# Gates and up projection of an encoder layer as seven products of halves

## The chip, the cores and the metric

One Trainium2 chip, one core of it. The time is the device time of one execution of the whole program in microseconds (us). TensorE (PE) does the matrix products, VectorE (DVE) and ScalarE (ACT) the arithmetic around them, GpSimd (POOL) some of it and the software DMA queue, SyncE (SP) issues most of the loads.

## The reference

Two groups of 256 tokens (512 in all, model width 1024) go through one encoder layer. Cut to what matters here:

```python
proj = rms_norm(x, norm1_g) @ w_in          # q, k, v of three branches, and three gates
qa, ka, va, qb, kb, vb, qm, ga, gb, gm = split(proj)
...                                         # attention branches oa, ob, om
merged = (sigmoid(ga) * (oa @ w_branch_a)
          + sigmoid(gb) * (ob @ w_branch_b)
          + sigmoid(gm) * (om @ w_branch_m))
x = x + merged @ w_out
h2 = rms_norm(x, norm2_g)
x = x + square(relu(h2 @ w_up)) @ w_down    # w_up 1024 x 4096, w_down 4096 x 1024
y = rms_norm(x, final_norm_g)
```

Each gate is a product 512 x 1024 by 1024 x 1024, the up projection one by 1024 x 4096. All of it is float32.

## The kernel before

**Precision by halves.** A float32 operand is split into a rounded part hi (ACT copies it into the type float32r) and a rest lo (DVE subtracts hi). `mm3` adds three products into one PSUM bank: hi by hi, hi by lo, lo by hi. Every weight tile `raw` or `blk` (128 x 1024 floats, 512 KB) so costs one ACT copy and one DVE subtraction before PE can use it.

**Units.** The program is a list of units that `run` emits in order; each has a function and the weights that it needs. Weights are fetched `ahead` weight tiles before their use (3 in the stages that matter here). The `lo` subtractions of a fetched tile are put into a list `lows`, which is emitted at the start of the next unit; what reads a product out of PSUM waits in a list `later`, which `flush` emits after the next product's matmuls. PE, ACT, DVE keep the order in which they were emitted; the order of DMAs on the SP and POOL queues is set by the scheduler.

**Gate stage.** Attention ends, then for each of eight blocks of 128 output features (`ff`): gate A and gate B, each `fm` with 8 contraction blocks of 128, 24 matmuls 128 x 512 (tokens are the 512 columns); then `branches`, the three branch products against OA, OB and OM (12, 6 and 12 matmuls), each multiplied by its gate on DVE and summed on POOL. The memory gate GM was computed earlier. `merge` splits the sums (tiles `mg`) for the output projection `out_proj`, which adds the residual and makes H, the normalised input of the MLP (up to the factor 1/rms, which comes in at the end).

**MLP.** The hidden width 4096 is walked in 8 columns `c` of 512. `up` makes a column of hidden features in 4 products of 24 matmuls 128 x 512, cut into 8 half units; in turns with them stand the seven products (P1, P2, Q5, Q6, P7, Q3, Q4) of the down projection of the column before, which is already written as seven products of halves instead of eight (12 matmuls 128 x 512 each). Its operands are sums of quarters of the weight: a tile T is changed in place by three accumulating DMAs on the POOL queue (`accum_op=add`), a tile C by one. Operands of tokens are made by `form` (DVE differences, ACT hi, DVE lo). Results go into accumulators by DVE (`acc`). Two products of a pair (P1 and P2, Q5 and Q3, P7 and Q4) share PSUM banks: the second adds to what the first left, after the first has been read.

In the profile almost every instruction of PE, ACT and DVE has line 72 (a helper); tiles tell them apart: `x` the normalised tokens, `g`, `q` gates, `w` weight halves, `h` H, `f` forms, `u` hidden features.

Of the kernel before, what the change touches and what calls it, by code (L numbers as in the profile page):

```python
# [16 lines left out]
P = 128  # L17
# [60 lines left out]
def encoder_kernel(ctx: ExitStack, tc: tile.TileContext, a: dict, out: bass.AP):  # L78
# [20 lines left out]
    def h2(s="h", dt=F32):  # L99
        return sb.tile([P, T], dt, tag="h2", name=nm(s), bufs=20)  # L100
# [10 lines left out]
    def f(x):  # L111
        return x.bitcast(F32)
# [86 lines left out]
    def fm(w, X, o):  # L199

        n = len(X)
        for k in range(n):
            c = slice(k * P, (k + 1) * P)
            mm3(o, w[0][:, c], w[1][:, c], X[k][:, 0], X[k][:, 1], k == 0, k == n - 1)
# [554 lines left out]
        unit(flush)  # L759


    MG, wb, sg = [], [], {}

    def gate(w, ff, br):
        p = bank()
        fm(w, X, p)
        g = h2("g")
        A.activation(g, p, AF.Sigmoid)
        sg[ff, br] = g

    def branches(w, *more):
        ff = len(MG)
        if more:
            wb[:] = more
        A.activation(GM[ff], GM[ff], AF.Sigmoid)
        sg[ff, 2] = GM[ff]
        c0 = (ff % 4) * 256
        parts = ((w[0][:, :512], w[1][:, :512], OA), (wb[0][0][:, c0:c0 + 256], wb[0][1][:, c0:c0 + 256], OB),
                 (w[0][:, 512:], w[1][:, 512:], OM))
        for br, (wh, wl, O) in enumerate(parts):  # L780
            p = bank()
            fm((wh, wl), O, p)
            V.tensor_tensor(sg[ff, br], p, sg[ff, br], op=ALU.mult)
        eng = V if ff == KD - 1 else G
        eng.tensor_tensor(sg[ff, 0], sg[ff, 0], sg[ff, 1], op=ALU.add)
        eng.tensor_tensor(sg[ff, 0], sg[ff, 0], sg[ff, 2], op=ALU.add)
        MG.append(sg[ff, 0])

    M = []

    def merge(*ks):
        for k in ks:
            x = s4("mg")
            A.activation(x[:, 0], MG[k], AF.Copy)
            (V, G)[k % 2 if k < KD - 1 else 0].tensor_tensor(x[:, 1], MG[k], f(x[:, 0]), op=ALU.subtract)
            M.append(x)

    for ff in range(KD):
        for br in range(2):
            unit(lambda w, ff=ff, br=br: gate(w, ff, br), (a["w_g"][ff, br],))  # L800
        if ff == KD - 1:
            unit(lambda: merge(*range(KD - 1)))
        unit(branches, (a["w_bam"][ff],), *([(a["w_bb"][ff // 4],)] if ff % 4 == 0 else []))


    unit(lambda: merge(KD - 1))


    X1, H = [], []

    def out_proj(w):
        ff = len(H)
        r = h2("xr")
        A.dma_start(r, a["xT"][:, ff])
        p = bank()
        fm(w, M, p)
        V.tensor_tensor(r, p, r, op=ALU.add)
        X1.append(r)
        x = s4("h")
        A.activation(x[:, 0], r, AF.Copy, scale=gains[:, 2, ff:ff + 1])  # L820
        V.scalar_tensor_tensor(x[:, 1], r, gains[:, 2, ff:ff + 1], f(x[:, 0]), op0=ALU.mult,
                               op1=ALU.subtract)
        H.append(x)

    for ff in range(KD):
        unit(out_proj, (a["w_o"][ff],))

# [74 lines left out]
    def load_blocks(c):  # L902

        if c in blocks:
            return
        t = {n: block_tile() for n in "T2BC"}
        for n, b in (("T", "11"), ("2", "21"), ("C", "12"), ("B", "22")):
            SP.dma_start(t[n], block(c, b))
        G.dma_start(t["C"], block(c, "22"), accum_op=ALU.add)
        blocks[c] = t  # L910

    def parts(c, n):

# [17 lines left out]
    def form(c, name):  # L931
# [9 lines left out]
        if name in ("P1", "P2", "Q4"):  # L941
            src = {"P1": A11, "P2": A12, "Q4": A22}[name]
        elif name == "Q5":
            src = forms[c, "S1"] = less(A21, A22)
        elif name == "Q6":
            src = forms[c, "S2"] = less(A11, forms.pop((c, "S1")))
        elif name == "P7":
            src = less(A11, A21)
        else:
            src = less(A12, forms.pop((c, "S2")))  # L950
# [8 lines left out]
    def add_to(k, i, p, op=ALU.add):  # L959
        if (k, i) in acc:  # L960
            V.tensor_tensor(acc[k, i], acc[k, i], p, op=op)
        else:
# [1 line left out]
            A.activation(acc[k, i], p, AF.Copy, scale=1.0 if op == ALU.add else -1.0)  # L964


    PRODUCTS = dict(P1=("T12", "a", "V", -1), P2=("2", "a", "11", 1), Q5=("T22", "d", "G", 1),
                    Q6=("T21", "c", "V", 1), P7=("C", "e", "G", -1), Q3=("B", "d", "12", 1), Q4=("T", "e", "21", 1))

    def product(w, c, name):  # L970
        _, bk, to, sign = PRODUCTS[name]
# [86 lines left out]
    unit(mlp_pool)  # L1058
    ORDER = ("P1", "P2", "Q5", "Q6", "P7", "Q3", "Q4")


    SUMMED = {1: ("12", "12"), 2: ("11", "11"), 3: ("21", "21"), 4: ("12", "V"), 5: ("21", "V", 1), 6: ("22", "G")}

    def make(c, n):
        unit(lambda: form(c, ORDER[n]))

    for c in range(NC):
        for h in range(8):
            ff, half = 4 * c + h // 2, h % 2
            unit(lambda *w, ff=ff, half=half: up(w[0] if w else None, ff, half), *([(a["w_up"][ff],)] if half == 0 else []))  # L1070
            if c == 0:
                unit(lambda h=h: turn_x1(h % 4, h // 4))
            if h == 1 and c < NC - 1:
                unit(lambda c=c: load_blocks(c))
            if h == 7 and c == NC - 2:
                unit(fetch_x1)
            if c == NC - 1 and h == 6:
                unit(lambda: ahead.__setitem__(0, 2))
            if c == NC - 1 and h in SUMMED:
                unit(lambda n=SUMMED[h]: later.append(lambda: combine(*n)))  # L1080
            if c and h < 7:
                for n in ((1, 2) if h == 0 else (h + 2,)):
                    if n < 7:
                        make(c - 1, n)
                unit(lambda w, c=c - 1, n=ORDER[h]: product(w, c, n), (parts(c - 1, PRODUCTS[ORDER[h]][0]),))
        if c == 0:
            unit(inv_ms)
            unit(lambda: ahead.__setitem__(0, 3))
        if c < NC - 1:
            make(c, 0)  # L1090
    unit(lambda *w: (kept.update({(0, 0): w[0], (1, 0): w[1]}), last_down(0, (0, 1))),
         *[(block(NC - 1, n),) for n in ("11", "21")])
    unit(lambda: later.append(lambda: combine("22", "V")))
# [84 lines left out]
```

## Time and profile before

| | us |
|---|---|
| median of 3 runs | 858.68 (857.31 to 859.06) |
| profiled execution | 859.08 |
| its span (first to last instruction) | 857.3 |
| PE busy in the span | 844.4 |
| DVE busy | 462.8 |
| ACT busy | 397.1 |
| POOL busy | 216.0 |

An instruction's duration includes the time until its last result is written, and the next one of the same engine begins before that; what one more instruction costs in a row is the distance between starts. The granted TensorE clock is 1.0 of full speed from 60 us on.

### The profile page before, as it was taken

How to read it: one execution, taken by the hardware profiler on the slowest of the kernel's cores; microseconds unless marked ns; L12 is line 12 of the kernel's file. 1: busy time of each engine (PE TensorE's matmuls, PEld its weight loads, DVE VectorE, ACT ScalarE, POOL GpSimd, SP SyncE). 2: the span in 40 equal slices, each digit the busy share in tenths (PEclk: the TensorE clock that was granted, in tenths of full speed). 3: DMA queues.
4: the chain of work that ended last, by engine and by line, in shares of the span. 5: the costliest groups of instructions: out<-in, count | busy, mean ns of one | idle time of the engine just before them, and what ended most of it. 6: DMA issues, size and time to landing. Idle time of an engine off the chain costs nothing.

```text
span 857.3 us, 10785 instructions
## 1 busy us (share of the span) xinstructions
PE 844.4 (99%) x4080; PEld 703.8 (82%) x4080; DVE 462.8 (54%) x737; ACT 397.1 (46%) x690; POOL 216.0 (25%) x161
## 2 busy tenths in 40 slices
PE   9999999999999999999999999999999999999996
PEld 7788998888888888888888788888888888888885
DVE  6575535465452311423435542465767666767895
ACT  6455545565554333222323227564445353545453
POOL 2314554656556543211123000000000000000001
PEclk9999999999999999999999999999999999999998
DMA  8343122324241228432322445374747465645322
GB/s 284 115 119 109 62 99 86 98 63 115 85 119 64 75 74 286 132 99 86 110 99 74 147 147 161 110 204 107 205 109 208 111 185 121 178 120 172 75 75 98
DMA packets 47468, 106.87 MB, mean 125 GB/s; under 512 B 19358, under 2 KB 19604, under 8 KB 47416
## 3 DMA queue, kind: packets, MB, share of 16 engines
q1 hardware_dynamic: 39992, 85.69, 30.2%
q0 software_dynamic: 4256, 14.73, 9.7%
q10 hardware_dynamic: 3168, 5.77, 2.0%
q8 instruction: 32, 0.52, 0.3%
q14 instruction: 20, 0.16, 0.1%
HBM read 101.93 MB, written 4.24 MB: 124 GB/s over the span
## 4 chain that ended last, share of the span: by engine, by line
PE 84%; DVE 8%; ACT 5%; issue 2%; DMA 1%; POOL 0%; POOLq 0%; SPq 0%; DVEq 0%; ACTq 0%
PE ps L72 77%; PE sc L72 3%; PE o L72 2%; DVE w L72 2%; PE tp L72 2%; ACT w L72 2%; DVE f L72 1%; ACT sp L72 1%; DVE sp L72 1%; DMA mr<-in_memT 1%; ACT f L72 1%; DVE sq L72 0%; ACT r L72 0%; DVE mg L72 0%; DVE acc L72 0%
## 5 line engine op out<-in xcount | busy, mean ns | idle before, releaser
L72 PE MATMUL ps<-x,w 128*128 128x512 f32 x1080 | 252.5, 391 | 0.0
L72 PEld LDWEIGHTS ps<-x,w 128*128 128x128 f32 x1080 | 201.0, 188 | 41.3
L72 PE MATMUL ps<-h,w 128*128 128x512 f32 x768 | 184.5, 391 | 0.0
L72 PEld LDWEIGHTS ps<-h,w 128*128 128x128 f32 x768 | 143.7, 188 | 29.5
L72 PE MATMUL ps<-w,f 128*128 128x512 f32 (+1 forms) x696 | 164.1, 387 | 1.3 <-DVE acc L72 1.0
L72 DVE TENSOR_TENSOR w<-raw,w 128x1024 fp32r<-128x1024 f32 (+1 forms) x79 | 96.4, 1223 | 115.3 <-ACT w L72 115.2
L72 PEld LDWEIGHTS ps<-w,f 128*128 128x128 f32 x696 | 128.7, 188 | 29.9 <-issue 3.4
L72 ACT ACTIVATE w<-raw 128x1024 fp32r<-128x1024 f32 (+2 forms) x116 | 119.7, 1036 | 21.9 <-DMA raw<-in_w_mem 7.5
L161 POOL TENSOR_TENSOR w<-raw,w 128x1024 fp32r<-128x1024 f32 (+1 forms) x37 | 87.3, 2361 | 120.1 <-ACT w L72 94.9
L72 DVE TENSOR_TENSOR w<-blk,w 128x1024 fp32r<-128x1024 f32 x49 | 59.5, 1224 | 47.7 <-ACT w L72 47.6
L923 POOL DMA_DIRECT2D blk<-in_w_dn x21 | 18.1, 864 | 240.2 <-DVE w L72 240.2
L72 ACT ACTIVATE w<-blk 128x1024 fp32r<-128x1024 f32 x49 | 50.7, 1047 | 15.4 <-DMA blk<-in_w_dn 15.4
L72 DVE TENSOR_TENSOR acc<-acc,ps 128x512 f32<-128x512 f32 x82 | 52.9, 682 | 2.9 <-PE ps L72 2.9
L72 ACT ACTIVATE f<-f 128x512 fp32r<-128x512 f32 x28 | 17.7, 633 | 75.4 <-DVE f L72 75.4
L72 ACT ACTIVATE sp<-sp,st 128x256 f32<-128x256 f32 (+1 forms) x48 | 25.8, 538 | 57.7 <-DVE st L72 57.7
L72 ACT ACTIVATE g<-ps 128x512 f32<-128x512 f32 x16 | 9.6, 598 | 88.4 <-PE ps L72 88.4
L72 DVE TENSOR_TENSOR sum<-o,lo 64x256 f32<-64x256 f32 x24 | 10.0, 417 | 66.5 <-ACT lo L72 66.3
L72 PE MATMUL ps<-mg,w 128*128 128x512 f32 x192 | 44.2, 391 | 1.5 <-ACT mg L72 0.9
L72 PEld LDWEIGHTS ps<-mg,w 128*128 128x128 f32 x192 | 36.0, 188 | 9.6 <-ACT mg L72 1.3
L72 ACT ACTIVATE r<-ps 128x512 f32<-128x512 f32 x32 | 18.9, 591 | 50.7 <-PE ps L72 50.7
L72 PE MATMUL ps<-w,x 128*128 128x384 f32 (+1 forms) x192 | 39.9, 363 | 0.0
L469 POOL TENSOR_TENSOR sp<-sp,st 128x512 f32<-128x512 f32 (+1 forms) x32 | 36.7, 1147 | 6.5 <-DVE st L72 3.6
(146 smaller groups left out, 959.2 us busy)
## 6 DMA issues: line engine op xcount, KB each, us to landing
raw<-in_w_up SPq DMA_DIRECT2D x32, 512.0 KB, 4.7
blk<-in_w_dn SPq DMA_DIRECT2D x28, 512.0 KB, 6.7
blk<-in_w_dn POOLq DMA_DIRECT2D x28, 512.0 KB, 5.7
raw<-in_w_g SPq DMA_DIRECT2D x24, 512.0 KB, 3.3
raw<-in_w_b SPq DMA_DIRECT2D x12, 512.0 KB, 3.3
raw<-in_w_bam SPq DMA_DIRECT2D x8, 512.0 KB, 3.3
raw<-in_w_o SPq DMA_DIRECT2D x8, 512.0 KB, 3.2
raw<-in_w_mem SPq DMA_DIRECT2D x7, 512.0 KB, 3.3
```

The costliest lines, as they stand in the source:

```text
L72: return self.tc.keep_in_program_order(method(*args, **kw))
L161: sub[0].tensor_tensor(lo[:, c], raw[:, c], f(hi[:, c]), op=ALU.subtract)
L469: G.tensor_tensor(s[:, :, :w], s[:, :, :w], st[:, 6:8].unsqueeze(2).to_broadcast([P, 2, w]), op=ALU.mult)
L923: G.dma_start(src, block(c, n[1:]), accum_op=ALU.add)
```

## The change

Gates A and B and columns 1 to 7 of the up projection are now seven products each, by one function `seven`. A block of 512 output features is cut into four quarters (contraction half by feature half), the tokens into two groups of 256, and one product multiplies 512 x 256 weights by 512 x 256 tokens: 2 x 4 x 3 = 24 matmuls, now with 256 columns. There are 4 such blocks for the gates (two halves of the features, A and B in turns) and 7 for the up projection. Column 0 of the up projection stays as it was.

- The token operands Q5, Q6, Q3 of X and of H are made once by `halves_of`, in eight pieces: DVE differences, ACT hi, DVE lo. The last two pieces overwrite half of X[0..3] or H[0..3] in place, for P7.
- Weight operands: T and C are loaded, then changed by accumulating DMAs (three on T, one on C); the quarters 21 and 22 come through `raw`. So each block loads 4 x 512 KB plainly and 4 x 512 KB with accumulation.
- The order of the seven is now P1, P2, Q5, Q3, Q6, P7, Q4, for the down projection too; its quarters 21 and 22 come through `raw` now.
- `take` reads the products out of PSUM: three copies by ACT, five sums by DVE per block, then sigmoid, or relu and square, by ACT.
- The memory branch is taken out of `branches` and stands first (`memory_branch`, eight units of 12 matmuls), with one piece of `halves_of` after each. The sums of branches go from POOL to DVE, in quarters of 256 tokens (`gated`). All of `merge` is on DVE. `out_proj` does its first two outputs together, contraction blocks 0 to 5 first.
- The pool that the weight blocks lie in takes over the attention's memory at the start of the gate stage, not at the start of the MLP.

```diff
+    SEVEN = ("P1", "P2", "Q5", "Q3", "Q6", "P7", "Q4")
+    ONTO = dict(P1="12", Q5="22", Q6="21")
+    BANK = dict(P1="a", P2="a", Q5="d", Q3="d", Q6="c", P7="e", Q4="e")
+    def halves_of(X, forms):
...
+        def less(x, y, out):
+            e = pair()
+            V.tensor_tensor(e, f(x), f(y), op=ALU.subtract)
+            V.tensor_tensor(out, e[:, 0], e[:, 1], op=ALU.add)
+        def minus(x, d, out):
+            V.tensor_tensor(out, f(x[:, 0]), d, op=ALU.subtract)
+            V.tensor_tensor(out, out, f(x[:, 1]), op=ALU.add)
+        def s1(j):
+            d = kept[1, j] = pair()
+            for i in range(2):
+                k = 2 * j + i
+                less(X[k][:, :, l], X[k + 4][:, :, l], d[:, i])
+            put("Q5", j, d)
...
+        def s3(j):
+            for i in range(2):
+                x, d = X[2 * j + i], pair()[:, 0]
+                less(x[:, :, u], x[:, :, l], d)
+                A.activation(x[:, 0, l], d, AF.Copy)
+                V.tensor_tensor(x[:, 1, l], d, f(x[:, 0, l]), op=ALU.subtract)
+        return [lambda fn=fn, j=j: fn(j) for fn in (s1, s2, s4_, s3) for j in range(2)]
...
+        def load():
+            t["T"], t["C"] = tiles()
+            SP.dma_start(by2(t["T"]), block("11"))
+            SP.dma_start(by2(t["C"]), block("12"))
+            G.dma_start(by2(t["C"]), block("22"), accum_op=ALU.add)
+        def weights(n):
+            hi, lo = w_tile(), w_tile()
+            if n in ("P2", "Q3"):
+                src = raw_tile()
+                SP.dma_start(by2(src), block("21" if n == "P2" else "22"))
+            else:
+                src = t["C" if n == "P7" else "T"]
+            A.activation(hi, src, AF.Copy)
+            def low():
+                V.tensor_tensor(lo, src, f(hi), op=ALU.subtract)
+                if n in ONTO:
+                    G.dma_start(by2(src), block(ONTO[n]), accum_op=ALU.add)
...
+            for j in range(2):
+                for k in range(4):
+                    c = slice(j * 512 + k * P, j * 512 + (k + 1) * P)
+                    xh, xl = form_of(X, forms, n, k)
+                    mm3(b[:, j * S:(j + 1) * S], w[0][:, c], w[1][:, c], xh, xl, new and j == k == 0, k == 3, j > 0 or not new)
+            flush(9)
+            later.append(lambda: take(n, b))
...
+            elif n == "Q6":
+                v = e["21"] = h2("e")
+                V.tensor_tensor(v, b, e["p"], op=ALU.subtract)
+                for m in ("12", "22"):
+                    V.tensor_tensor(e[m], e[m], v, op=ALU.add)
+                put("12", e["12"])
...
+    def gated(ff, br, p):
+        for i in range(2):
+            c, x = slice(i * S, (i + 1) * S), sg[ff, br, i]
+            V.tensor_tensor(x, p[:, c], x, op=ALU.mult)
+            V.tensor_tensor(MG[ff][:, c], MG[ff][:, c], x, op=ALU.add)
...
+    for ff in range(KD):
+        unit(memory_branch, (lambda ff=ff: half_chunk(a["w_bam"][ff][:, 512:]),))
+        unit(pieces[ff])
+    for q in range(2):
+        for n in range(7):
+            for br in range(2):
+                unit(g4[q, br][1][n][0], g4[q, br][1][n][1])
...
     for c in range(NC):
-        for h in range(8):
-            ff, half = 4 * c + h // 2, h % 2
-            unit(lambda *w, ff=ff, half=half: up(w[0] if w else None, ff, half), *([(a["w_up"][ff],)] if half == 0 else []))
+        for n in range(7 if c else 0):
+            unit(*u7[c][1][n])
+            if c == 1 and n in (1, 2):
+                unit(pieces_up[5 + n])
+            if n == 1 and c < NC - 1:
+                unit(lambda c=c: load_blocks(c))
+            if n == 3 and c < NC - 1:
+                u7[c + 1] = up_seven(c + 1)
+                unit(u7[c + 1][0])
...
+            down_unit(c - 1, n)
```

**PE, gate A.** In the rows below a name is a tile with its number; `ps` is a PSUM bank, `x` a tile of tokens (hi and lo), `w` the hi or lo half of a weight tile, the first two of a group of three having the same weights. Before, the start of the first gate product after the attention:

```order
L72 MATMUL ps_3151<-x_442,w_3038 128x512 x2
L72 MATMUL ps_3151<-x_442,w_3039 128x512
L72 MATMUL ps_3151<-x_458,w_3038 128x512 x2
L72 MATMUL ps_3151<-x_458,w_3039 128x512
L72 MATMUL ps_3151<-x_462,w_3038 128x512 x2
L72 MATMUL ps_3151<-x_462,w_3039 128x512
```

Now, the start of P1 of gate A, behind the last memory branch:

```order
L72 MATMUL ps_3374<-om_1228,w_3302 128x512 x2
L72 MATMUL ps_3374<-om_1228,w_3303 128x512
L72 MATMUL ps_3406<-x_442,w_3329 128x256 x2
L72 MATMUL ps_3406<-x_442,w_3330 128x256
L72 MATMUL ps_3406<-x_458,w_3329 128x256 x2
L72 MATMUL ps_3406<-x_458,w_3330 128x256
```

The gate product behind the attention gave way to the memory branches, and the matmuls that follow are half as wide.

**DVE, start of the gate stage.** Before, DVE has the subtractions of the weights (`w`) and one multiplication per branch (`g`, `q`):

```order
L72 TENSOR_TENSOR w_3375<-raw_3373,w_3374 128x1024
L72 TENSOR_TENSOR w_3408<-raw_3406,w_3407 128x1024
L72 TENSOR_TENSOR w_3441<-raw_3439,w_3440 128x1024
L72 TENSOR_TENSOR g_3404<-ps_3446,g_3404 128x512
L72 TENSOR_TENSOR g_3437<-ps_3460,g_3437 128x512
L72 TENSOR_TENSOR q_2865<-ps_3468,q_2865 128x512
```

Now, at the end of the memory branches (`q` the branch times its gate, `d` the differences of a piece, `x` the half of X that is overwritten, the last `w` that of P2 of gate B):

```order
L72 TENSOR_TENSOR q_3116<-ps_3342,q_3116 128x512
L72 TENSOR_TENSOR w_3389<-raw_3390,w_3388 128x1024
L72 TENSOR_TENSOR d_3395<-x_462 128x512
L72 TENSOR_TENSOR d_3394<-d_3395 128x256
L72 TENSOR_TENSOR x_462<-d_3394,x_462 128x256
L72 TENSOR_TENSOR d_3401<-x_466 128x512
L72 TENSOR_TENSOR d_3400<-d_3401 128x256
L72 TENSOR_TENSOR x_466<-d_3400,x_466 128x256
L72 TENSOR_TENSOR q_3149<-ps_3374,q_3149 128x512
L72 TENSOR_TENSOR w_3433<-raw_3434,w_3432 128x1024
```

The weights that the gate products need now stand behind the pieces in DVE's queue.

**POOL, one column of the MLP.** Before, the three accumulations on T (line 923) stand together, and the one on the next column's C (line 909) behind them:

```order
L923 DMA blk_4989<-in_w_dn 128x1024 x3
L909 DMA blk_5618<-in_w_dn 128x1024
L923 DMA blk_5302<-in_w_dn 128x1024 x3
L909 DMA blk_5931<-in_w_dn 128x1024
L923 DMA blk_5615<-in_w_dn 128x1024 x3
```

Now (lines 861 and 1114 on T of the up and the down projection, 847 and 1096 on C):

```order
L1096 DMA blk_6150<-in_w_dn 128x1024
L847 DMA blk_6272<-in_w_up 128x2x512
L861 DMA blk_5861<-in_w_up 128x2x512
L1114 DMA blk_5739<-in_w_dn 128x1024
L861 DMA blk_5861<-in_w_up 128x2x512
L1114 DMA blk_5739<-in_w_dn 128x1024
L861 DMA blk_5861<-in_w_up 128x2x512
L1114 DMA blk_5739<-in_w_dn 128x1024
```

A column has eight accumulations where it had four, and the two on the next column's C stand ahead of the first on this column's T.

More of the change, by code (lines that the diff above doesn't have):

```diff
@@ L759, in encoder_kernel, with late_pool, block_tile @@
         unit(flush)
-    MG, wb, sg = [], [], {}
-    def gate(w, ff, br):
-        p = bank()
[L766 to L772, printed above, removed]
+    def late_pool():
+        stages.close()
+        at[0] = stages.enter_context(tc.tile_pool(name="ml", bufs=1))
+    def block_tile():
+        return at[0].tile([P, 1024], F32, tag="blk", name=nm("blk"), bufs=8)
+    SEVEN = ("P1", "P2", "Q5", "Q3", "Q6", "P7", "Q4")
@@ L780, in branches @@
-        for br, (wh, wl, O) in enumerate(parts):
+        for br, (wh, wl, O) in enumerate(((*w, OA), (*(x[:, c0:c0 + 256] for x in wb[0]), OB))):
             p = bank()
             fm((wh, wl), O, p)
[L783 to L787, printed above, removed]
+            flush(9)
+            later.append(lambda br=br, p=p: gated(ff, br, p))
@@ L826, in encoder_kernel @@
+    unit(out_proj, *[(a["w_o"][ff],) for ff in range(2)])
+    for ff in range(2, KD):
         unit(out_proj, (a["w_o"][ff],))
@@ new lines, in start_up, with up_seven, block, put @@
+    def start_up():
+        for n in ("Q5", "Q6", "Q3"):
+            HF[n] = [sb.tile([P, 1024], F32R, tag="s4", name=nm("f"), bufs=21) for _ in range(2)]
+    def up_seven(c):
+        def block(n):
+            k, f0 = int(n[0]) - 1, 4 * c + 2 * (int(n[1]) - 1)
+            return a["w_up"][f0:f0 + 2, :, k * 512:(k + 1) * 512].rearrange("f p c -> p f c")
+        def put(n, x):
+            i, h = int(n[0]) - 1, int(n[1]) - 1
+            if (c, h) not in UP and c < NC - 1:
+                UP[c, h] = sb.tile([P, 2, T], F32, tag="s4", name=nm("u"), bufs=21)
+            r = h2("r") if n == "11" else x
+            A.activation(r, x, AF.Relu)
+            if c == NC - 1:
+                return put_last(i, h, r)
+            A.activation(UP[c, h][:, :, i * S:(i + 1) * S], r.rearrange("p (j t) -> p j t", j=2), AF.Square)
+        return seven(H, HF, block, lambda: (block_tile(), block_tile()), put)
@@ new lines, in make, with down_unit @@
+    def make(c, n):
+        unit(lambda: form(c, SEVEN[n]))
+    def down_unit(c, n):
+        for m in ((1, 2) if n == 0 else (n + 2,)):
+            if m < 7:
+                make(c, m)
+        unit(lambda w: product(w, c, SEVEN[n]), (parts(c, PRODUCTS[SEVEN[n]][0]),))
+    pieces_up = halves_of(H, HF)
+    for h in range(8):
+        ff, half = h // 2, h % 2
+        unit(lambda *w, ff=ff, half=half: up(w[0] if w else None, ff, half), *([(a["w_up"][ff],)] if half == 0 else []))
+        unit(lambda h=h: turn_x1(h % 4, h // 4))
+        if h == 0:
+            unit(start_up)
+        if h < 6:
+            unit(pieces_up[h])
+        if h == 1:
+            unit(lambda: load_blocks(0))
+            u7[1] = up_seven(1)
+            unit(u7[1][0])
@@ L1078, in encoder_kernel @@
                 unit(lambda: ahead.__setitem__(0, 2))
[L1079 to L1085, printed above, removed]
+            if c == NC - 1 and n in SUMMED:
+                unit(lambda n=SUMMED[n]: later.append(lambda: combine(*n)))
```

201 lines of the change are left out of this document (151 added, 50 removed).

## The prediction

> **What bounds the kernel now.** I read the page's busy table first, then PE's waits, then PE's groups by shape.
>
> ```profile
> PE 844.4 (99%) x4080; PEld 703.8 (82%) x4080; DVE 462.8 (54%) x737; ACT 397.1 (46%) x690; POOL 216.0 (25%) x161
> PE ps L72 <- DVE acc L72: 1.0, 6, 0.2
> PE ps L72 <- ACT mg L72: 0.9, 1, 0.9
> PE ps L72 <- DVE mg L72: 0.6, 1, 0.6
> L72 PE MATMUL ps<-x,w 128*128 128x512 f32 x1080 | 252.5, 391 | 0.0
> L72 PE MATMUL ps<-h,w 128*128 128x512 f32 x768 | 184.5, 391 | 0.0
> ```
>
> PE has work 99% of the span, and its longest waits sum to 2.5 us, 1.5 of them at the output projection (`mg`). So the time is the number of matmuls times their distance, plus whatever new waits come in. DVE at 54% is no bound on the average; it may be in a stage, since it takes its queue in order.
>
> What one matmul costs is the distance between starts, read from a timeline of PE (start, duration, group):
>
> ```profile
> 73.25 5.63 PE L72 MATMUL ps<-x,w 128*128 128x512 f32 x24
> 78.72 0.88 PE L72 MATMUL sc<-mk,qm 128*128 128x256 f32 x6
> 79.43 5.63 PE L72 MATMUL ps<-x,w 128*128 128x512 f32 x24
> 91.50 0.88 PE L72 MATMUL o<-pT,mv 128*128 128x256 f32 x6
> 92.21 0.60 PE L72 MATMUL tp<-ident,sp 128*128 128x128 f32 x4
> 61.66 11.04 PE L72 MATMUL ps<-x,w 128*128 128x512 f32 x48
> 72.53 0.88 PE L72 MATMUL sc<-mk,qm 128*128 128x256 f32 x6
> L72 PE MATMUL ps<-w,f 128*128 128x256 f32 x24 | 3.0, 283 | 0.0
> ```
>
> With 512 columns: (72.53 - 61.66) / 48 = 0.2265 us. With 256 columns: (79.43 - 78.72) / 6 = 0.118, (92.21 - 91.50) / 6 = 0.118; the 24 at the end of the kernel take 3.0 us together, 0.125 with the last one's tail and (3.0 - 0.28) / 23 = 0.118 without. Half the columns cost 0.52 of the time, not 0.50. I take 0.1195, between 0.118 and 0.125 and near the first; new weights for each matmul are in all these rows.
>
> **The change on PE.** Counted in the program: 384 matmuls `ps<-x,w` and 672 `ps<-h,w` of 512 columns go, 1848 of 256 columns come (11 blocks x 7 x 24). Off: 1056 x 0.2265 = 239.2. On: 1848 x 0.1195 = 220.8. Gain 18.4 us (bounds: 21.1 at 0.118, 8.2 at 0.125). The eighth saved by seven of eight (30 us) loses 12 us to the fixed part of each matmul. The memory branches and the other branch products are only moved.
>
> The Trainium skill ("TensorE: Matmul & The Clock Gate", Back-to-back issue gap) gives N/2.4 + 2.5 ns, so 109 ns for 256 columns and 216 for 512; by it the gain would be an estimated 26 us. The rows show 118 and 226.5, some 10 ns more on each, and the measurement decides.
>
> **What the new work costs DVE.** The rows for its prices (durations, and starts for pairs):
>
> ```profile
> 652.79 1.28 DVE L72 TENSOR_TENSOR acc<-acc,ps 128x512 f32<-128x512 f32 x2
> 656.60 2.36 DVE L72 TENSOR_TENSOR w<-blk,w 128x1024 fp32r<-128x1024 f32 x2
> 797.27 1.41 DVE L72 SCALAR_TENSOR_TENSOR blk<-acc,rr,blk 128x512 f32<-128x512 f32 x2
> 795.28 0.69 DVE L72 TENSOR_TENSOR f<-u,f 128x512 f32<-128x512 f32 x1
> 796.66 0.69 DVE L72 TENSOR_TENSOR f<-f,f 128x512 fp32r<-128x512 f32 x1 [0.70 <-ACT f L72]
> L72 DVE TENSOR_TENSOR om<-o,om 128x256 fp32r<-128x256 f32 x8 | 3.4, 425 | 16.3 <-ACT om L72 16.3
> L72 ACT ACTIVATE om<-o 128x256 fp32r<-128x256 f32 x8 | 3.1, 383 | 6.5 <-PE o L72 6.4
> L72 ACT ACTIVATE w<-raw 128x1024 fp32r<-128x1024 f32 x110 | 115.1, 1050 | 19.9 <-DMA raw<-in_w_mem 5.6 <-DMA raw<-in_w_bam 5.6 <-DMA raw<-in_w_a 3.9
> 842.97 0.15 DVE L72 TENSOR_REDUCE fr<-fs 128x1 f32<-128x2 f32 x1 [0.79 <-ACT junk L72]
> 843.16 0.15 DVE L72 TENSOR_SCALAR fr<-fr 128x1 f32<-128x1 f32 x1
> 747.00:788.30 41.30, 41.13 (x182) 33.77 (x181) 28.39 (x36) 19.39 (x27) 2.59 (x3) 1.00 0.53 145
> 788.30:829.00 40.70, 40.53 (x180) 33.30 (x179) 35.25 (x48) 19.37 (x27) 1.72 (x2) 1.00 0.32 80
> ```
>
> In a row of independent ones, 512 elements cost 0.60 (1.28 less the first 0.69), 1024 cost 1.13, a scaled sum 0.66, 256 an estimated 0.34 (0.425 less the same 0.09). If an instruction reads the one before, nothing overlaps (842.97 + 0.15, then 843.16): 0.71 and 0.45. If ACT's hi stands between two of them, DVE idles 0.70 (0.45 for 256 elements, from the 383 ns). The last two rows are stretches of one column (length, PE, PE loads, DVE, ACT, POOL, clock, DMA share, GB/s).
>
> *Memory branches.* PE needs 12 x 0.2265 = 2.72 us for each and 2.86 for a gate product; DVE has per branch a multiplication, a subtraction of weights and a piece. Pieces: Q5 0.71 + 0.34 + 0.71 + 0.43 + 0.70 + 0.60 = 3.5; Q6 and Q3 0.45 + 0.34 + 0.45 + 0.43 + 0.70 + 0.60 = 3.0; P7 2 x (0.71 + 0.43 + 0.45 + 0.34) = 3.9. From the end of the first branch's product to the weights of P2 of gate B, all in one queue: 8 multiplications and 4 half subtractions, 12 x 0.60 = 7.2; 4 whole ones, 4.5; pieces 3.5 + 4 x 3.0 + 2 x 3.9 = 23.3. Sum 35.0. PE has 7 x 2.72 + 3 x 2.86 = 27.6 until it wants them. PE waits 7 us at P1 of gate B and both P2 (bounds 2, if the 5 x 0.70 + 4 x 0.45 = 5.3 us of idling behind ACT were not there, and 9 with two ACT copies late by one weight, 1.05). Behind P2 the pieces are gone, DVE has 1.13 per 2.86, and nothing waits.
>
> *End of the gate stage.* From the product with OA of `ff` 4 to contraction block 5 of the output projection PE has 75 x 0.2265 = 17.0 us. DVE has 7 groups of `gated` (2 x (0.45 + 0.34) = 1.6), 2 x 0.60 + 3 x 1.13 for weights and 6 splits of 0.60: 19.4. Late 2.4 where the two `mg` rows above show 1.5: +0.9 (bounds -1.5 and +3).
>
> *Columns 2 to 6.* PE: 7 x (24 x 0.1195 + 12 x 0.2265) = 39.1 us. DVE: the 28.4 above, + 3 more weights (3.4) + 5 sums (3.0) = 34.8, and some 4 waits of 0.70 for forms are idle in between already: some 36 to 37.5 of 39.1. No wait of PE, but the cover is 2 us where it was 10. Column 1 has the two P7 pieces of H too (7.7), less its first sums (ACT copies those), with six pieces of H queued from column 0: I take 1.5 us of waiting, bounds 0 and 4.
>
> *Column 7.* Until Q4 of the down product may add to P7's banks, PE has 39.1 us from the end of column 6's last up product. DVE has 13 weights (14.7), 12 scaled sums (7.9), 25 of 512 (15.0), 6 of 256 (2.0), three waits for a form (2.4), one for relu, square and copy (1.1): 43.1. PE waits 4 us (bounds 0.5 and 6). The row of 788.30 shows where it comes from: 35.25 of 40.7 before, and 7 us of work on top with 1.6 us less time.
>
> *ACT.* 19.4 a column, + 3 weights (3.0) + 3 copies (1.8): 24 of 39. Not the bound; it is in order too, so a late DMA holds all that stands behind it. *POOL* loses its sums; only DMA issues are left.
>
> *DMA.*
>
> ```profile
> q1 hardware_dynamic: 39992, 85.69, 30.2%
> q0 software_dynamic: 4256, 14.73, 9.7%
> blk<-in_w_dn POOLq DMA_DIRECT2D x28, 512.0 KB, 5.7
> ACT w L72 <- DMA blk<-in_w_dn: 15.4, 7, 3.3
> ```
>
> Of 16 engines' time, a plain 512 KB costs 0.302 x 857.3 x 0.524 / 85.69 = 1.58 us, an accumulating one 0.097 x 857.3 / 28 = 2.97. A column before: 8 plain and 4 accumulating, 24.5 of 41.3, 0.59. Now 8 and 8: 36.4 of 39.1, 0.93, at this price, which has contention in it. An accumulation lands in 5.7 us; from P1's subtraction to ACT's copy for Q5 there are four units, 11 us, so 4 us are to spare for POOL's queue, where two accumulations on C now stand ahead. I cost it at 0 on PE, hidden by the three weights fetched ahead, and put its failure among the rivals. The gate blocks have the same density and no forms on DVE.
>
> **Sum**, against the profiled execution's 859.1 (span 857.3 and 1.8 around it; 0.4 above the median): 859.1 - 18.4 + 7 + 0.9 + 1.5 + 4 = 854.1; on the median's scale 854.
>
> **Rivals.** *DVE's queue costs little* (the waits are half mine or less: DVE starts pieces while PE is still in the last memory gate product, ACT's copies fall into other work). For it: before, no wait over 0.2 us on `acc`, even in the 35.25 of 40.7. Against: sums of 35 against 27.6 leave no way around. 859.1 - 18.4 + 2 = 843; 840 to 849.
>
> *Slower: accumulations arrive late in every column.* Mechanism: the DMA engines at 0.93 make T land later than 11 us after P1's subtraction; ACT's copy waits with everything behind it, DVE waits for ACT, and DVE's 2 us of cover per column are gone. It decides from some 2 us of DVE idling per column. The 15.4 us in 7 waits show that ACT already waits 2.2 us a column on the old order, with no cost to PE; against: the new order leaves two more units between T's uses. If T is 4 us later in 6 columns and 4 gate blocks, half of it reaching PE: 854 + 10 x 2 = 874 at worst, 866 with 1.2 us each. This alone makes the kernel slower.
>
> *Weight loads bound it.* A load is recorded with 188 ns against 118 for 256 columns; if they were serial, 1848 x 0.07 = 129 us more. The six-row groups above have a load each and still step by 0.118: excluded, 1 in 100. The Trainium skill (same page, LDWEIGHTS) has 128/1.2 = 107 ns per load, just below the step, which agrees with the rows.
>
> *It doesn't do what it says*: excluded by the order, 1056 matmuls against 1848.
>
> **Chances.** My forecast (849 to 861) 0.52, little waiting 0.21, late accumulations (861 to 875) 0.25, rest 0.02. Range 844 to 866: a tenth each side is left out. A difference within 0.2% (1.7 us) can't be told from none: faster means below 857.0: 0.21 + 0.41 of the forecast's 0.52 = 0.62; same, 857.0 to 860.4: 0.12; slower 0.26.
>
> **What the profile after should show.** PE's groups with 256 columns, 1848 in all, 0.118 to 0.120 apart. PE's waits: on DVE `w` around the first gate products, 5 to 8 us together; on `mg` 2 to 3; in column 7 on `acc`, `e` or `w`, 3 to 5. DVE over 90% busy in column 7, some 88 to 92% in columns 2 to 6, with no PE wait there over 0.5 us a column. DMA share 0.8 to 0.95 in the columns, accumulations landing in 6 to 9 us. I am wrong if matmuls of 256 columns with `w` as weights step by 0.125 or more, if ACT waits for `blk` over 4 us a column, or if DVE's waits for ACT in steady columns reach PE.

## The result, and the profile after

| | before | after |
|---|---|---|
| median | 858.2 us (857.3 to 859.1) | 929.6 us (927.0 to 931.0) |
| ratio | | 1.083, 95% interval 1.080 to 1.086 |
| span of the profiled execution | 857.3 | 929.3 |
| PE idle in the span | 12.9 | 78.3 |

The kernel became 71 us slower, where 4 us of gain had been forecast. From the page of the profile after, PE's busy time, its granted clock in 40 slices, and the two DMA queues:

```profile
PE 851.0 (92%) x4872; PEld 737.2 (79%) x4872; DVE 592.3 (64%) x973; ACT 459.1 (49%) x788; POOL 235.4 (25%) x185
PEclk9999999999999997999989999799999999999999
q1 hardware_dynamic: 46776, 85.69, 27.9%
q0 software_dynamic: 16224, 37.80, 24.1%
```

Of the 72.0 us of span, 65.4 are PE idle (78.3 less 12.9). The other 6.6 are PE busy: by the forecast's count it should have fallen by 18.4, so 25 us of matmul time are extra. Most of that is the clock: its granted mean over the span is 0.973 where before had 0.993, so 0.027 x 929.3 = 25.1 us went by it against 0.007 x 857.3 = 6.0, some 19 us more. The rest, an estimated 6 us, are ends of matmuls: the last one ahead of a wait counts with its full length (24 of them last 3.04 us by themselves and are 24 x 0.1195 = 2.87 apart, so 0.17 each), and the trace has 51 stops of PE where before had 13. Four rows of PE show what follows a wait (start, duration, group, the wait ahead of it in brackets):

```profile
366.93 7.55 PE L72 MATMUL ps<-x,w 128*128 128x256 f32 x48 [6.96 <-ACT e L72]
586.55 5.49 PE L72 MATMUL ps<-f,w 128*128 128x256 f32 x24 [8.33 <-ACT e L72]
714.42 4.63 PE L72 MATMUL ps<-h,w 128*128 128x256 f32 x24 [2.12 <-ACT e L72]
856.58 3.14 PE L72 MATMUL ps<-h,w 128*128 128x256 f32 x24 [2.13 <-ACT e L72]
```

Twenty-four of these take 3.14 us at full clock (last row) and 5.49 behind a wait of 8.33. The third row lost 1.5 us behind a wait of 2.12, the fourth, the same product three columns later behind the same wait, lost nothing. The granted clock in these four stretches is 0.76, 0.50, 0.63 and 1.00. So a wait of some 2 us is followed by a slow stretch only now and then.

The Trainium skill ("TensorE: Matmul & The Clock Gate", Part 1: The HAM clock gate, and HAM oscillation) says that an idle window of about 3.4 us halves the clock and that about 3.4 us of work bring it back. The rows behind 7 and 8 us agree; the third row shows a loss behind a shorter wait, which follows other waits of 1 to 2 us.

PE's waits in two stretches, first around the start of the gate products (330 to 400 us, four rows), then over the MLP (545 to 905 us, four rows): total, times, longest:

```profile
PE ps L72 <- ACT e L72: 7.0, 1, 7.0
PE ps L72 <- ACT w L72: 3.1, 4, 1.1
PE ps L72 <- DVE w L72: 1.8, 4, 0.8
PE ps L72 <- DVE e L72: 0.7, 1, 0.7
PE ps L72 <- ACT e L72: 21.4, 9, 8.3
PE ps L72 <- DVE e L72: 13.8, 6, 3.6
PE ps L72 <- DVE acc L72: 10.2, 10, 2.3
PE ps L72 <- ACT f L72: 4.7, 1, 4.7
```

PE waits 50 us in the MLP, where before had 1.3 (`acc`). A column of the MLP (third and fourth row of the fence before: the same product, three columns apart) takes (856.58 - 714.42) / 3 = 47.4 us; 39.1 was forecast. What happens in a pair of units is read from the timeline of DVE, ACT and PE, from the sum behind one P7 to the sum behind the next product, Q4:

```profile
698.40 0.68 DVE L72 TENSOR_TENSOR e<-e,ps 128x512 f32<-128x512 f32 x1
699.11 0.63 ACT L72 ACTIVATE e<-e 128x512 f32<-128x512 f32 x1 [3.27 <-DVE e L72]
699.22 3.10 PE L72 MATMUL ps<-h,w 128*128 128x256 f32 x24 [2.21 <-DVE e L72]
699.77 0.63 ACT L72 ACTIVATE u<-e 128x512 f32<-128x512 f32 x1
700.31 1.99 ACT L72 ACTIVATE w<-blk 128x1024 fp32r<-128x1024 f32 x2
701.39 1.23 DVE L72 TENSOR_TENSOR w<-blk,w 128x1024 fp32r<-128x1024 f32 x1 [2.31 <-ACT w L72]
702.53 1.28 DVE L72 TENSOR_TENSOR acc<-acc,ps 128x512 f32<-128x512 f32 x2
703.36 3.00 PE L72 MATMUL ps<-w,f 128*128 128x512 f32 x12 [1.04 <-DVE acc L72]
703.73 1.22 DVE L72 TENSOR_TENSOR w<-blk,w 128x1024 fp32r<-128x1024 f32 x1
704.86 0.68 DVE L72 TENSOR_TENSOR e<-ps,e 128x512 f32<-128x512 f32 x1
705.58 0.63 ACT L72 ACTIVATE e<-e 128x512 f32<-128x512 f32 x1 [3.28 <-DVE e L72]
```

This is a ring. DVE's sum `e` lets ACT do relu (`e<-e`) and square (`u`), behind which stands the hi of the next weights (`w<-blk`); behind that hi DVE has the lo (`w`), the accumulators (`acc`), another lo, and then the next `e`. From start to start: 0.71 + 0.66 + 0.54 + 1.08 + 1.14 + 1.20 + 1.13 = 6.46 us, against 5.59 that PE needs for the pair. In each turn DVE idles 2.31 us for ACT and ACT 3.3 us for DVE. Neither is busy; each has a queue in order, and each has put the piece that the other wants behind a piece that waits for the other.

### The profile page after: what moved, and what is told of

Read it like the earlier page. It is cut to its first block, busy times and chain, and to the rows that moved or that the text cites. A ratio compares the mean times of both kernels' runs of the same rounds, so it can differ in the third digit from the quotient of the medians.

```text
span 929.3 us, 12847 instructions
## 1 busy us (share of the span) xinstructions
PE 851.0 (92%) x4872; PEld 737.2 (79%) x4872; DVE 592.3 (64%) x973; ACT 459.1 (49%) x788; POOL 235.4 (25%) x185
## 4 chain that ended last, share of the span: by engine, by line
DVE 22%; PE 13%; ACT 11%; issue 10%; DMA 7%; POOL 1%; POOLq 0%; ACTq 0%; DVEq 0%; SPq 0%
PE ps L72 13%; DVE w L72 7%; ACT w L72 6%; DVE acc L72 4%; DMA blk<-in_w_dn 4%; DVE f L72 3%; DVE e L72 3%; DVE d L72 2%; ACT e L72 2%; ACT f L72 2%; DMA blk<-in_w_g 1%; DVE blk L72 1%; DVE q L72 1%; ACT r L72 1%; DMA wb<-in_w_g 1%
## 5 line engine op out<-in xcount | busy, mean ns | idle before, releaser
L72 PE MATMUL ps<-x,w 128*128 128x512 f32 (+1 forms) x1080 | 215.4, 357 | 11.8 <-ACT e L72 7.0
L72 PEld LDWEIGHTS ps<-x,w 128*128 128x128 f32 x1080 | 178.2, 193 | 40.0 <-ACT e L72 7.3
L72 PE MATMUL ps<-h,w 128*128 128x256 f32 (+1 forms) x768 | 117.3, 312 | 26.9 <-DVE e L72 13.8
L72 PEld LDWEIGHTS ps<-h,w 128*128 128x128 f32 x768 | 107.6, 204 | 37.1 <-issue 16.7
L72 DVE TENSOR_TENSOR w<-raw,w 128x1024 fp32r<-128x1024 f32 (+1 forms) x82 | 90.9, 1114 | 61.5 <-ACT w L72 60.6
L72 DVE TENSOR_TENSOR w<-blk,w 128x1024 fp32r<-128x1024 f32 x75 | 91.7, 1222 | 49.7 <-ACT w L72 49.7
L72 PE MATMUL ps<-f,w 128*128 128x256 f32 x792 | 100.8, 286 | 8.6 <-ACT e L72 8.5
L72 PEld LDWEIGHTS ps<-f,w 128*128 128x128 f32 x792 | 99.2, 194 | 11.7 <-ACT e L72 10.5
L861 POOL DMA_DIRECT2D blk<-in_w_up x21 | 27.9, 1328 | 247.1 <-DVE w L72 236.0
L72 ACT ACTIVATE w<-blk 128x1024 fp32r<-128x1024 f32 x75 | 76.0, 1048 | 8.7 <-DMA blk<-in_w_dn 7.6
L72 ACT ACTIVATE e<-e 128x512 f32<-128x512 f32 x36 | 22.8, 632 | 98.1 <-DVE e L72 98.0
```

The lines of the kernel that those rows point to most:

```text
L72: return self.tc.keep_in_program_order(method(*args, **kw))
L861: G.dma_start(by2(src), block(ONTO[n]), accum_op=ALU.add)
```

## The experiments

Theory 1: the ring, together with pieces of `halves_of` that stand ahead of the first products' copies. Theory 2: accumulating transfers land late. Ratios are to before, with 95% intervals.

**One half of the change each.** `e1_gates` has the gates of the change and the MLP of before, `e2_up` the opposite.

```diff
# e1_gates: everything from NC = 8 on as before; e2_up: the gate stage and out_proj as before
-        for n in range(7 if c else 0):
-            unit(*u7[c][1][n])
+        for h in range(8):
+            unit(lambda *w, ff=ff, half=half: up(w[0] if w else None, ff, half), ...)
```

> Only the gates of A and B go as seven products; the up projection and the blocks of the down projection are as before. TensorE by the pitches of the traces: 384 x 0.2265 off, 672 x 0.1195 on, -6.7 us. Theory 1 (two in-order queues, ACT and DVE, wait for each other's pieces) puts 15.4 us of waits into the gate stage and some 4 us into the merge after it, with about 10 us lost to the half clock behind them: 858 - 7 + 20 + 10 = 881, between 872 and 888. Theory 2 (accumulating transfers come too late) has its places in the columns of the MLP, and gives 860 to 870 here.

> Only the up projection goes as seven products; the gates are as before. TensorE: 672 x 0.2265 off, 1176 x 0.1195 on, -11.7 us. Both theories have the waits in the columns: 56 us more of them than before, and some 14 us at half clock: 858 - 12 + 56 + 14 = 916, between 905 and 925. With the run of the gates alone this tells whether the two losses add up to the 71 us of the whole change.

Measured: 875.7 us (1.021, 1.019 to 1.023) and 910.3 us (1.061, 1.059 to 1.063). 18.3 and 52.9 us lost, together 71.2: the losses are separate and add up. `e1_gates` came out in theory 1's range. `e2_up` is in the range that both theories share and doesn't tell them apart.

**Breaking the ring.** `e3_defer` has the whole change with the same instructions; only ACT's part behind the sum is put into `later`.

```diff
                 for m in ("12", "22"):
                     V.tensor_tensor(e[m], e[m], v, op=ALU.add)
-                put("12", e["12"])
+                later.append(lambda: put("12", e["12"]))     # likewise "22" behind P7, "21" behind Q4
```

> The whole change, and the same instructions, but behind the last three products of each seven the relu and square (or the sigmoid) of the finished sum are put on ACT's queue one product later, behind the rounding of the next weights. DVE then need not wait for ACT to have waited for DVE. Theory 1: a column falls from about 46 us to 40 or 41, with most of the half clock gone from the columns: 885 to 905. Theory 2: the transfers are where they were, nothing changes by more than 5 us: 925 to 932.

Measured: 905.5 us (1.057, 1.054 to 1.059): 24 us won by order alone, half a microsecond above the range for the ring and 20 below that for the transfers. The waits that are left, in PE's rows of Q3 and ACT's waits in the MLP:

```profile
632.09 3.14 PE L72 MATMUL ps<-f,w 128*128 128x256 f32 x24 [2.21 <-ACT e L72]
766.08 4.63 PE L72 MATMUL ps<-f,w 128*128 128x256 f32 x24 [3.24 <-ACT e L72]
ACT w L72 <- DMA blk<-in_w_dn: 28.6, 5, 6.6
```

A column now takes (766.08 - 632.09) / 3 = 44.7 us. ACT's waits for `blk` of `in_w_dn`, 7.6 us over the MLP in the profile after, have grown to 28.6: with the ring gone, DMA is next.

**Leaving out the accumulations** of the gates and the up projection (`e4_noacc`), the ring left in.

```diff
-            G.dma_start(by2(t["C"]), block("22"), accum_op=ALU.add)
...
-                if n in ONTO:
-                    G.dma_start(by2(src), block(ONTO[n]), accum_op=ALU.add)
```

> The whole change without the accumulating transfers of the gates' and the up projection's blocks (the four sums of blocks are left out of the weights, so the result is another one; every instruction of PE, ACT and DVE stays). Theory 1: the ring of ACT and DVE stays, 915 to 930. Theory 2: the columns no longer wait for sums that arrive late, 870 to 895.

Measured: 926.7 us (1.080, 1.079 to 1.082), 3 us less than the whole change, although ACT has no wait for `blk` left in the MLP (8.6 us in the profile after, `in_w_dn` and `in_w_up` together). As long as the ring stands, these transfers cost next to nothing; those of the down projection stayed in.

**A first try at POOL's order** (`e5_pool`), on top of `e3_defer`: the accumulation onto C becomes a unit of its own, `join`, two or three products later.

```diff
-                unit(u7[c + 1][0])
+                unit(u7[c + 1][0][0])
+            if n == 5 and c < NC - 1:
+                unit(lambda c=c: join_blocks(c))
+            if n == 6 and c < NC - 1:
+                unit(u7[c + 1][0][1])
```

> As e3_defer, and the accumulating transfer of block 22 onto C, which waits on POOL's queue for the plain load ahead of it, is issued two or three products later (the load of its C stays where it was), so that the accumulations onto T no longer stand behind it. In e3_defer a column lost 2.4 to 3.4 us to one accumulation onto T that was issued some 4 us late and landed after 10 us. If the order on POOL is the cause: those waits go, five columns by some 2.8 us and a little clock, 888 to 896. If the transfers are late because the DMA engines are full, the order changes nothing: 901 to 908.

Measured: 907.5 us (1.058, 1.056 to 1.061): no change. This did not decide: C still stood ahead of one accumulation onto T on POOL, since the order of DMAs is the scheduler's.

**Spreading the pieces** of `halves_of` (`e6_pieces`), on the change itself, and all three edits together (`e7_all`).

```diff
-        unit(pieces[ff])
+        if ff % 2:
+            unit(pieces[ff // 2])
...
+                if q == 0 and 2 * n + br in PIECE:          # {0: 4, 2: 5, 4: 6, 5: 7, 6: 8, 7: 9}
+                    unit(pieces[PIECE[2 * n + br]])
...                                                          # and the rounding of a piece in `later`
-            if c == 1 and n in (1, 2):
-                unit(pieces_up[5 + n])
+            if c == 1 and 0 < n < 4: ...
```

> The changed kernel, with the sums of quarters for the forms of X and H spread out: in the gate stage four of them beside the memory branch, the others beside the first four pairs of products, and in column 1 beside products 2 to 4; each rounding (ACT's copy and DVE's rest) one unit behind the sums it rounds. Same work. If the 15 us of waits in the gate stage and the 13 us ahead of and in column 1 come from pieces that stand ahead of the first products' copies on ACT's and DVE's queues, most of them go, with the half clock behind them: 898 to 910. If DVE's work itself is too much there, the waits come a few products later: 920 to 930.

> Late activations, POOL's order and spread pieces together, same work as the changed kernel. If the three losses are separate, the gains add: 930 - 24 - 13 - 25 = 868, between 858 and 878. If DVE's work (36 to 37 of some 39 us of TensorE's a column) is the next bound, the columns stay at 42 us or more: 880 to 895. If all waits went, the sum of the prediction's TensorE term alone, 840, would come out.

Measured: 918.9 us (1.071, 1.070 to 1.073) and 890.8 us (1.039, 1.037 to 1.040). Alone the pieces win 11 us, less than the 20 to 32 I gave them; with the ring broken 15 to 17. `e7_all` came out in the range that I had written for DVE's work as the next bound; the next pair of runs shows that it was not DVE. What the pieces did is seen in the change's own trace at P2 of gate A, whose bank waits for the copy of P1 (`e<-ps`):

```profile
363.85 0.69 DVE L72 TENSOR_TENSOR d<-x 128x512 f32<-128x512 f32 x1
364.57 0.43 DVE L72 TENSOR_TENSOR d<-d 128x256 f32<-128x256 f32 x1
365.03 0.42 ACT L72 ACTIVATE x<-d 128x256 fp32r<-128x256 f32 x1 [1.55 <-DVE d L72]
365.35 1.04 ACT L72 ACTIVATE w<-raw 128x1024 fp32r<-128x1024 f32 x1
366.30 0.58 ACT L72 ACTIVATE e<-ps 128x512 f32<-128x512 f32 x1
```

P1 had long been done. The copy stood on ACT's queue behind the rounding of the last piece, and that one waited for DVE's queue of pieces: PE waited 6.96 us (the first row of the clock's fence).

**POOL's order, enforced** (`e8_order`), and as its bound all accumulations left out (`e9_noacc`), both on `e7_all`.

```diff
+        def join():                                # a unit behind product P2 of the block's own seven
+            with tc.issue_after(lastT[0].ins):     # the last accumulation onto a T
+                G.dma_start(by2(t["C"]), block("22"), accum_op=ALU.add)
```

> As e7_all, and the accumulations of block 22 onto C are bound by an edge of order behind the two accumulations onto T that follow Q5's weights, so that on POOL's queue no accumulation onto T stands behind a C that waits for its plain load. (e5_pool meant to do this and did not: POOL's order kept the C ahead of an accumulation onto T, and its time was that of e3_defer.) In e7_all a column still takes 44 us, 2.3 to 3.4 of them one wait for a T that was issued 3 to 6 us late and landed after 10 to 11 us; the gate stage has one wait of 5.2 us of that kind. If the order on POOL is the cause: 870 to 880. If the DMA engines themselves are full: 886 to 892.

> As e7_all, with all accumulating transfers of the gates, the up and the down projection left out (the sums of blocks are missing from the weights, so the result is another one; every instruction of PE, ACT and DVE stays). This is the end of what any order of the accumulations could win. If the transfers are what is left once ACT and DVE no longer wait for each other: 860 to 875, while leaving out those of gates and up alone won only 3 us in the changed kernel itself (e4_noacc). If DVE's work is what is left: 882 to 890.

Measured: 866.5 us (1.011, 1.010 to 1.013) and 863.7 us (1.007, 1.006 to 1.009). The order on one queue is worth 24 us here (the time is 3.5 us under the range that was given for it), and is within 3 us of having no accumulations at all. Four rows of `e7_all`, POOL's issues (idle time in brackets) and those who want the tile:

```profile
639.10 1.21 POOL L849 DMA_DIRECT2D blk<-in_w_up  x1 [3.15 <-DMA blk<-in_w_up]
639.82 1.43 POOL L1126 DMA_DIRECT2D blk<-in_w_dn  x1
650.52 1.06 ACT L72 ACTIVATE w<-blk 128x1024 fp32r<-128x1024 f32 x1 [6.17 <-DMA blk<-in_w_dn]
658.92 1.33 PE L72 MATMUL ps<-f,w 128*128 128x256 f32 x9 [3.21 <-ACT e L72]
```

The accumulation onto C (L849) waits 3.15 us for its plain load, T (L1126) issues behind it and lands 10.7 us later; ACT idles 6.17 us for it, and all that stands behind on ACT is late, up to PE. The same place in `e8_order`, with two rows of the same product three columns apart, ACT's waits for these tiles over the MLP (first `e7_all`, then `e8_order`), and one stretch of 40 us in `e8_order` and in the profile after (length, PE, PE loads, DVE, ACT, POOL, clock, DMA share, GB/s):

```profile
642.37 0.91 POOL L1129 DMA_DIRECT2D blk<-in_w_dn  x1 [0.66 <-DVE w L72]
642.94 1.57 POOL L852 DMA_DIRECT2D blk<-in_w_up  x1
643.66 1.79 POOL L1112 DMA_DIRECT2D blk<-in_w_dn  x1
648.01 2.00 ACT L72 ACTIVATE w<-blk 128x1024 fp32r<-128x1024 f32 x2
627.12 3.11 PE L72 MATMUL ps<-h,w 128*128 128x256 f32 x24 [0.44 <-DVE e L72]
746.32 3.10 PE L72 MATMUL ps<-h,w 128*128 128x256 f32 x24 [0.16 <-DVE e L72]
ACT w L72 <- DMA blk<-in_w_dn: 27.6, 5, 6.6
ACT w L72 <- DMA blk<-in_w_dn: 0.2, 1, 0.2
640.00:680.00 40.00, 39.85 (x257) 36.10 (x256) 34.95 (x46) 23.84 (x32) 8.74 (x9) 1.00 0.87 211
640.00:680.00 40.00, 35.68 (x217) 31.86 (x216) 29.33 (x38) 21.91 (x30) 6.36 (x6) 0.96 0.79 182
```

T (L1129) now goes ahead of both accumulations onto C (L852, L1112) and lands 6.2 us after its issue; ACT does not wait for it. A column takes (746.32 - 627.12) / 3 = 39.7 us, PE is busy 39.85 of 40 us with DVE at 34.95 and the DMA engines at 0.87, as forecast for columns 2 to 6; only column 6 still has a wait of 1.7 us.

**The same order without the other two edits** (`e12_orderonly`).

> The changed kernel with nothing but the order of e8_order on POOL's queue (activations and pieces as in the changed kernel). In e7_all that order was worth 24 us. If the ring of ACT and DVE hides the late transfers in the changed kernel, as e4_noacc says (3 us without the accumulations of gates and up): 922 to 930. If late transfers were a loss of their own from the start: 900 to 912.

Measured: 931.4 us (1.086, 1.084 to 1.088), nothing won. Two rows of PE three columns apart, and ACT's waits for DVE's sums over the MLP:

```profile
716.71 4.46 PE L72 MATMUL ps<-h,w 128*128 128x256 f32 x24 [2.13 <-ACT e L72]
855.44 3.14 PE L72 MATMUL ps<-h,w 128*128 128x256 f32 x24 [2.08 <-ACT e L72]
ACT e L72 <- DVE e L72: 74.3, 21, 4.7
```

ACT has no wait for `blk` left here, but its waits for DVE's sums, three a column, are those of the change to the tenth (74.3 us there, and in `e4_noacc`). A column takes (855.44 - 716.71) / 3 = 46.2 us with the ring alone, 44.7 with the late transfers alone (`e3_defer`), 47.4 with both (the change) and 39.7 with neither (`e8_order`). So the two causes don't add: the ring hides the late transfers, and breaking the ring shows them.

**What was left** at Q4 and at the ends of the stages.

```diff
# e10_p7
-                V.tensor_tensor(e["22"], e["22"], b, op=ALU.subtract)
+                copy("7")                                    # by ACT, out of the bank that Q4 adds to
+                V.tensor_tensor(e["22"], e["22"], e["7"], op=ALU.subtract)
# e11_ends, beside it
-            V.tensor_tensor(MG[ff][:, c], MG[ff][:, c], x, op=ALU.add)
+            (G if 3 < ff < 6 else V).tensor_tensor(MG[ff][:, c], MG[ff][:, c], x, op=ALU.add)
...                                                          # and pieces and forms moved, as said below
```

> As e8_order, and P7 is copied out of its bank by ACT, as P1, Q5 and Q3 are, and subtracted from the copy by DVE; Q4, which adds to the same bank, then waits for ACT's copy and not for DVE's subtraction. One ACT copy of 128x512 more per seven (0.58 us), 11 in all. In e8_order TensorE waits 14.1 us for DVE's e, at Q4 of both halves of the gates (3.8 and 3.0), of columns 1, 6 and 7 (3.0, 1.7, 1.7). If DVE's queue is what holds Q4: 855 to 861. If ACT stands behind DVE there anyway: 864 to 868.

> As e10_p7, and at the ends of the stages: six of the ten pieces of X's forms go beside the memory branch and four beside the first two pairs of products (before: four and six); for two chunks of the second half of the merge POOL adds the gated branches, not DVE; in column 1 the form of P1 is made one unit earlier, and the forms of P2 and Q5 behind the first product of the down projection. In e8_order these places cost 2.3 us (merge), 1.2 and 2.2 us (column 1) and part of 3.8 us (gates). If DVE's and ACT's queues there are the cause: 4 to 8 us less than e10_p7, 848 to 856, so not slower than before. If POOL's adds or the earlier pieces only move the waits: within 3 us of e10_p7.

Measured: 863.6 us (1.006, 1.004 to 1.008; its runs spread from 859.8 to 868.5) and 864.4 us (1.008, 1.007 to 1.010). The copy won some 3 us, less than expected and between its two ranges; the edits at the ends won nothing, as was expected if the waits only move.

**Where the rest sits.** `e14_up` is the MLP of `e10_p7` with the gates of before, `e15_gates` the opposite, and `e13_cols` has the seven only in columns 2 to 7.

> e10_p7's MLP with the gates and the merge as before: TensorE -11.7 us against waits of 15.1 us in the MLP of e10_p7 (before: 2.4), with some 2 us at half clock: 858 to 862. With e2_up (910) it says how much of the up projection's loss the four repairs take away.

> e10_p7's gates with the MLP as before: TensorE -6.7 us against waits of 9.0 us in the gate and merge stages of e10_p7 (before: 1.9), with some 2 us at half clock: 857 to 862. With e1_gates (876) it says how much of the gates' loss the repairs take away.

> The up projection alone in seven products, in columns 2 to 7 only, with late activations, the order on POOL, the pieces of H's forms beside column 1 and the first products of column 2, P7 copied by ACT, and the last column's rests of LAST on POOL except the first pair; gates, column 0 and column 1 as before. TensorE: 576 x 0.2265 off, 1008 x 0.1195 on, -10.0 us. If what is left in e10_p7 sits at the entrance into the sevens (column 1: 7.4 us), in the gates (9) and in the last column (4.7): some 3 us of waits remain and the time is 849 to 855, faster than before. If the pieces and the heavier DVE make the same waits wherever the sevens begin: 857 to 862.

Measured: 862.7 us (1.005, 1.003 to 1.007), 862.7 us (1.006, 1.004 to 1.007) and 870.0 us (1.013, 1.011 to 1.016). Each half keeps 4 to 5 us of loss, just above what was expected. `e13_cols` missed: it started the sevens a column later and found longer waits there, up to 3.7 us, with the pieces of H beside it again. That fits an entrance that costs wherever the pieces meet a stage that needs DVE; no run separates this from its other edits.

**Making the entrance cheap** (`e16_entry`): three pieces of H go into the output projection's stage, the sums of the others beside column 0, only four roundings into column 1. Beside that, the first forms are made earlier and the last column's rests go to POOL; the run doesn't separate these.

```diff
+        if ff == 5:
+            unit(lambda: start_up("Q5", "Q6"))
+            unit(lambda: pieces_up[0]())
+        if ff == 6:
+            unit(lambda: pieces_up[2]())
+        if ff == 7:
+            unit(lambda: pieces_up[1]())
...
+            if c == 1 and n < 4:
+                unit(pieces_up[10 + n])                      # ACT's hi and DVE's lo only
```

> As e14_up (gates as before), with the entrance into the columns eased: three pieces of H's forms are made in the output projection's stage, where DVE is idle half of the time, the sums of all others beside column 0, only four roundings (0.42 us each on ACT and DVE) in column 1; the form of P1 one unit earlier, those of P2 and Q5 behind the first product; the last column's rests on POOL except the first pair. e14_up waits 7.3 us in column 1 and 3.5 us in the last one. If DVE's work at the entrance is what is left: 854 to 859, no longer slower than before. If the last column or the output stage takes the wait over: 860 to 864.

Measured: 855.6 us in 9 runs, before 857.4 in 14 (0.9976, 0.9965 to 0.9988). This version, up projection alone with all repairs, is faster than before by 0.24%, and so faster than both kernels. Its page and one stretch of its columns:

```profile
PE 833.7 (98%) x4584; PEld 716.6 (84%) x4584; DVE 526.2 (62%) x833; ACT 435.9 (51%) x753; POOL 256.1 (30%) x195
630.00:670.00 40.00, 39.92 (x255) 36.19 (x254) 34.95 (x45) 24.33 (x33) 8.53 (x9) 1.00 0.86 211
```

PE's busy time is 844.4 - 833.7 = 10.7 us below before, where the count gives 1176 matmuls on and 672 off, 152.2 - 140.5 = 11.7. Waits of PE still take most of it back.

## Why the prediction was wrong

**The matmuls** were right. 24 of 256 columns and 12 of 512 were given 5.59 us; with nothing in the way, in `e8_order`, a column of seven pairs takes 39.7 us, 39.1 forecast. `e16_entry`'s PE time confirms the gain to 1 us. The 109 and 216 ns that I took from the Trainium skill ("TensorE: Matmul & The Clock Gate", Back-to-back issue gap) are there the gap of a single matmul by itself; for a stream the page has about 131 ns with 512 columns. Neither is what the rows show, 226.5, and the sum went by the rows.

**The step that failed is that of columns 2 to 6, "No wait of PE, but the cover is 2 us where it was 10".** These columns took 47.4 us where 39.1 were forecast, so an estimated 40 us of the 76 by which the sum was short lie in these five. Its terms were right: 34.8 us of DVE work forecast, 34.95 in the stretch of `e8_order`. The reasoning was not. I summed DVE's work against PE's and put ACT aside ("24 of 39. Not the bound"), with a late DMA as the only thing that could hold it. But `take` made DVE's results an input of ACT, on a queue on which DVE's own next inputs stood behind. Two queues that are 73% and 55% busy (29.33 and 21.91 of 40 us in the last row of that fence) then went round in 6.46 us where PE needs 5.59; seven such rounds would be 45.2 us, and `e12_orderonly`, where only the ring is left, has 46.2 a column. The sign was in the forecast, as what would prove it wrong: "if DVE's waits for ACT in steady columns reach PE". They did. I had it as a sign to look for and gave it neither a rival nor a price.

**Memory branches, +7**: the sum of DVE's queue was of the right kind but not complete. Waits of PE between 330 and 400 us were 12.6 us (7.0 + 3.1 + 1.8 + 0.7), and the largest came at P2 of gate A by way of ACT: its copy of P1 stood behind the rounding of a piece. A piece was priced on DVE alone; it has an instruction on ACT, too, and every one of those waits for DVE. The same thing happened a second time, with 8.33 us, in column 1, for which I had taken 1.5.

**DMA, 0 on PE**: the cover was counted as 11 us of distance against 5.7 of landing, 4 to spare for POOL's queue (11 less 5.7 is 5.3). The trace of `e7_all` showed 10.7 us of landing behind a C that had waited for its plain load. In the changed kernel the up projection's and the gates' part of this cost 3 us (`e4_noacc`), and the order nothing (`e12_orderonly`), since the ring was slower; without the ring it cost 24 (`e7_all` to `e8_order`). So the slower rival, late accumulations, was a true mechanism with a price somewhat too low (7 to 20 us); alone it would have made the kernel slow, but in the change the ring was slower and hid it. The measured 930 us are far above the 861 to 875 that it had been given.

**The clock** had no term. Some 19 us of the 72 are matmuls at a lower clock. That it comes from the waits was not tried by itself; it went with them: by the mean granted clock 25.1 us with 78 us of PE idle (the change, 0.973), 10.4 with 33 (`e8_order`, 0.988), 4.3 with 20 (`e16_entry`, 0.995), where before has 6.0 with 13.

**End of the gate stage (+0.9)**: 3.2 us of waiting on `mg` where before had 1.5, +1.7, inside its bounds. **Column 7 (+4)** can't be told from the ring in the change; in `e14_up` PE waits 2.8 us on `acc` there. The two rivals that were excluded stayed so, and the one on the faster side fell: DVE's queue did cost.

## What to carry to other kernels

Sum each engine's work against the bound, but also follow a result around: where engine X waits for Y and Y's next input stands behind X's waiting instruction, the loop's length, not either engine's busy time, is the pace. Put what waits (an activation of a fresh sum, a DMA that needs another DMA) behind what does not on every in-order queue; here such moves, without one instruction less, took 62 of 71 us away (`e8_order`). Repair one such cause and look again before judging the next: the second was worth 3 us before the first was repaired and 24 after.

## What the runs showed of the hardware that I had not expected

A single wait of PE of 2.1 us can be followed by a slow clock (24 matmuls in 4.63 us instead of 3.14, granted clock 0.63 in that stretch), and in the next three columns the same wait is not. An accumulating transfer of 512 KB lands late when it is issued 0.7 us behind another one: in `e7_all` five such T landed after 9.8 to 11.3 us, one a column, and the others of that line between 560 and 790 us after 5.1 to 6.9. In `e8_order`, with the DMA engines at 0.87 of their time instead of 0.79 (the stretch from 640 to 680 us in both), the T of the down projection take 5.7 to 11.1, and the C that now goes last takes 10.6 to 12.0, for which nobody waits. So the transfers did not become faster; the order chose which of them was late. At a share of 0.87 columns 2 to 5 ran with no wait of PE over half a microsecond; the 0.93 that I had feared for the whole change is not reached.
